# The first weight tile in halves of 256 columns, and GpSimd's bias tables placed behind the splits of x

## The chip, the core and the metric

The kernel runs on one core of a Trainium2 chip. The metric is the device time of one execution in microseconds, smaller is better. The engines of the core work side by side, each through its own list of instructions in order: TensorE (PE: matmuls, PEld: its weight loads), VectorE (DVE), ScalarE (ACT), GpSimd (POOL) and the DMA queues that ScalarE and SyncE (SP) issue to.

## The reference

One decoder layer on x (256 tokens, 1024 channels), all in float32:

```python
h = rms_norm(x, norm_g)
q, k, v, gate = split(h @ w_in, 4)          # w_in: 1024 x 4096
o = causal_attention(q, k, v, alibi)        # 16 heads of 64
x = x + (o * silu(gate)) @ w_out            # w_out: 1024 x 1024
return rms_norm(x, final_norm_g)
```

With 256 tokens there is one attention block of 256, so the block selection of the reference is plain causal attention with a linear distance penalty per head (ALiBi).

## The kernel before

**Split products.** TensorE multiplies in a reduced float32 format. To keep float32 accuracy each operand a is split into a high part (a rounded to that format) and a low part (a minus the high part), and a product is three matmuls: high·high, low·high, high·low. For weights ScalarE writes the high part `whi` by a copy, VectorE subtracts for the low part `wlo`. For x the transposed input `head` is scaled by the norm's gain: the high part `xh` is made by VectorE for k tiles 0 and 1 and by ScalarE for 2 to 7, the low part `xl` by VectorE in one instruction with two tensor inputs.

**Staging.** The 1024 input channels are 8 k tiles of 128. The weights come in pieces of 128 x 1024 elements. Pieces 0 to 3 hold the first half of the columns of v, two k tiles each (512 columns per k tile); later pieces hold 256 columns of q, k or the gate, four k tiles each. Four buffers hold weights as loaded, four their high parts and four their low parts.

**The first stage (v).** `run_first` multiplies all 8 k tiles into two banks: per k tile 6 matmuls of 512 columns. It picks the next matmul by a planner (`Plan`) that models when operands come, and before the first real one it issues warm-up matmuls on zeros (`warm_to`). The lists of all engines are fixed when the program is built.

**The norm's row scale.** h's division by the row norm is applied after the products. While the first stages run, ScalarE squares and sums two tiles of x (256 x 1024), VectorE turns each sum into a mean (`ms`), and GpSimd raises it to the power -1/2 (`rstd`, one instruction of 128 x 1 for each of the two row tiles). VectorE spreads each `rstd` along a diagonal (`spread`), TensorE transposes the two spread tiles (in the midst of the q matmuls), and ScalarE copies the result out as `rows`, with which q, k and the gate are scaled on their way out of their banks.

**The bias tables.** GpSimd computes the ALiBi penalty of each of the 16 heads, 128 x 256 elements (`make_bias`, one instruction per head from the table `dist`). The tables are first read by the softmax of the first head pair, after 33 us.

**Queues at the start.** ScalarE issues two transfers before its first instruction, SyncE all the others, in a written order. Lines that matter: `load` (172) and the calls at 182 to 188, `split_hi`/`split_lo` (230, 243), `make_bias` (218, called at 554), `root` (527, GpSimd's power at 534), `x_lo` (547), `v_first` (578), `fiber_norm` (602, the spread at 615).

Of the kernel before, what the change touches and what calls it, by code (L numbers as in the profile page):

```python
# [8 lines left out]
F32 = mybir.dt.float32  # L9
F32R = mybir.dt.float32r  # L10
AF = mybir.ActivationFunctionType
ALU = mybir.AluOpType

P = 128
S = 256
D = 1024
H = 16
DH = 64
NM = S // P
NK = D // P  # L20
CW = 512
GW = 256
KP = 4
# [9 lines left out]
N_PIECES = N_IN + NK  # L33


LAID = [("x", 0, 1), ("w", 0, 0, 2), ("x", 1, 2), ("w", 0, 1, 2)]
for c in range(1, NK // 2):
    LAID += [("x", 2 * c, 2 * c + 2), ("w", c, 0, 2), ("w", c, 1, 2)]
LAID += [("w", NK // 2, 0, 1)] + [("t", m) for m in range(NM)]
LAID += [("w", i, 0, 1) for i in range(NK // 2 + 1, N_PIECES)]  # L40
WIDTH, START = {}, {}
for seg in LAID:
    START[seg] = P * sum(WIDTH.values())
# [16 lines left out]
NL = 4  # L60
# [22 lines left out]
def f32(ap):  # L83
    return ap.bitcast(F32)
# [3 lines left out]
def trunk(ctx: ExitStack, tc, laid, fin_g, out):  # L88
    nc = tc.nc
    plan = Plan()  # L90
    const = ctx.enter_context(tc.tile_pool(name="const", bufs=1))
    w32p = ctx.enter_context(tc.tile_pool(name="w32p", bufs=NL))
    whp = ctx.enter_context(tc.tile_pool(name="whp", bufs=NW))
    wlp = ctx.enter_context(tc.tile_pool(name="wlp", bufs=NW))
# [11 lines left out]
    def mm(o, a, b, start, stop, n, dep=0.0):  # L106
        nc.tensor.matmul(o, a, b, start=start, stop=stop)  # L107
        return plan.mm(n, dep)
# [5 lines left out]
    def act(o, i, fn, n, dep, psum_in, scale=1.0, bias=0.0, accum=None):  # L114
        kw = {} if accum is None else {"accum_out": accum}
        if not isinstance(bias, float):
            kw["bias"] = bias
        nc.scalar.activation(o, i, fn, scale=scale, **kw)  # L118
        c = (50 if psum_in else 92) + n / 1.2
        c += 93 * ((not isinstance(scale, float)) + (not isinstance(bias, float)) + (accum is not None))  # L120
        return plan.op("act", c, dep)

    def dve(n, dep, rate=0.96, extra=0):
        return plan.op("dve", 66 + extra + n / rate, dep)
# [24 lines left out]
    gT, sg = head[:, :NK], head[:, NK:].rearrange("p (k n) -> p k n", k=NK)  # L149

    x_at, xt_at = [0.0] * NM, [0.0] * NK
    w32, whi, wlo, w_at, w_ready = {}, {}, {}, {}, {}
    dma = [1600.0]

    def fetch(o, seg, queue=None, dep=0.0):
        n = P * WIDTH[seg]
        (queue or nc.sync).dma_start(o, laid[START[seg]:START[seg] + n].rearrange("(p n) -> p n", p=P))
        dma[0] = max(dma[0], dep) + n / 90.0
        return dma[0] + LAT

    def load_x(m):

        x_at[m] = fetch(xs[m], ("t", m))

    def load_xt(k0, k1, queue=None):

        o = head[:, (NK + k0 * S if k0 else 0):NK + k1 * S]
        at = fetch(o, ("x", k0, k1), queue)
        for k in range(k0, k1):
            xt_at[k] = at  # L170

    def load(i, parts=1, dep=0.0, part=None, queue=None):
        if i >= N_PIECES:
            return
        if not part:
            w32[i] = w32p.tile([P, KP * GW], F32, name="w32")
            w_at[i] = []
        n = KP * GW // parts
        for u in range(parts) if part is None else [part]:
            w_at[i].append(fetch(w32[i][:, u * n:(u + 1) * n], ("w", i, u, parts), queue, dep))  # L180

    load_xt(0, 1)
    load(0, 2, part=0, queue=nc.scalar)
    load_xt(1, 2, nc.scalar)
    load(0, 2, part=1)
    for c in range(1, NK // 2):
        load_xt(2 * c, 2 * c + 2)
        load(c, 2)
# [1 line left out]

    ident = const.tile([P, P], F32, name="ident")
    make_identity(nc, ident)
    mhalf = const.tile([P, 1], F32, name="mhalf")
    nc.gpsimd.memset(mhalf, -0.5)
    dist = const.tile([P, S], F32, name="dist")
# [6 lines left out]
    x_hl = [const.tile([P, NK * S], F32R, name=f"x{t}") for t in "hl"]  # L202
    xh, xl = [[t[:, k * S:(k + 1) * S] for k in range(NK)] for t in x_hl]
# [14 lines left out]
    def make_bias(h):  # L218
        slope = -(2.0 ** (-8.0 * (h + 1) / H))
        nc.gpsimd.tensor_scalar(bias[:, h, :], dist, slope, 0.0, op0=ALU.mult, op1=ALU.add)  # L220


    nsplit = [0, 0]
    used_at = {}

    def rel(i):

        return used_at.get(N_IN if i == N_PIECES - 1 else i - NW + 1, 0.0) + 250.0

    def split_hi(parts=1, part=None):  # L230
        i = nsplit[0]
        if not part:
            whi[i] = x_hl[0][:, :KP * GW] if i == N_PIECES - 1 else whp.tile([P, KP * GW], F32R, name="whi")
            w_ready[i] = []
        n = KP * GW // parts
        for u in range(parts) if part is None else [part]:
            c = slice(u * n, (u + 1) * n)
            at = w_at[i][(u + 1) * len(w_at[i]) // parts - 1] if parts <= len(w_at[i]) else w_at[i][-1]
            w_ready[i].append(act(whi[i][:, c], w32[i][:, c], AF.Copy, n, max(at, rel(i)), False))
        if part is None or part == parts - 1:  # L240
            nsplit[0] += 1

    def split_lo(parts=None, part=None):
        i = nsplit[1]
        if not part:
            wlo[i] = x_hl[1][:, :KP * GW] if i == N_PIECES - 1 else wlp.tile([P, KP * GW], F32R, name="wlo")
        parts = parts or len(w_ready[i])
        n = KP * GW // parts
        for u in range(parts) if part is None else [part]:
            c = slice(u * n, (u + 1) * n)  # L250
            nc.vector.tensor_sub(wlo[i][:, c], w32[i][:, c], f32(whi[i][:, c]))  # L251
            w_ready[i][u] = dve(n, max(w_ready[i][u], rel(i)))
        if part is None or part == parts - 1:
            nsplit[1] += 1
            load(i + NL, 1, w_ready[i][-1] + 1100.0)

    used = [0, 0.0]

    def use(i):
        for u in range(used[0] + 1, i + 1):  # L260
            used_at[u] = plan.pe
        used[0] = i
        used[1] = plan.pe
        fill()
# [239 lines left out]
    with tc.manual_schedule():  # L504
# [10 lines left out]
        def warm_to(t):  # L515

            while plan.pe + 430.0 < min(t, WARM_END):
                warm(1)
# [18 lines left out]
        x_at_k = {}  # L537
# [11 lines left out]
                                           op0=ALU.mult, op1=ALU.subtract)  # L549
            x_at_k[k].append(dve(S, x_at_k[k][0], extra=62))  # L550

        whi_at = {}

        for h in range(H):
            make_bias(h)
        warm_to(3480.0)
        acc = banks[4:6]
        for b in acc:
            b["busy"] = True
        for c in range(NK // 2):  # L560
            for a in range(2):
                x_hi(2 * c + a, "act" if c else "dve")
                split_hi(2, a)
                x_lo(2 * c + a)
                whi_at.setdefault(c, []).append(w_ready[c][a])
                split_lo(2, a)
            if c == 0:
                load_x(0)
                load_x(1)

        def term(m, k, jj):
            i, a = divmod(k, 2)
            w_at_k = (whi_at if jj < 2 else w_ready)[i][a * len(w_ready[i]) // 2]
            return max(w_at_k, x_at_k[k][jj == 1])

        done = {0: 0, 1: 0}

        def v_first(m, k, jj):
            i, a = divmod(k, 2)
            xx, ww = ((xh, whi), (xl, whi), (xh, wlo))[jj]  # L580
            n = done[m]
            done[m] += 1
            return mm(acc[m]["t"], xx[k][:, m * P:(m + 1) * P], ww[i][:, a * CW:(a + 1) * CW], n == 0, n == 3 * NK - 1,
                      CW, term(m, k, jj))

        def run_first(todo, end=1e9):
            while todo and plan.pe < end:
                u = next((u for u in todo if term(*u) <= plan.pe), None) or min(todo, key=lambda u: term(*u))
                if term(*u) > end:
                    return  # L590
                warm_to(term(*u))
                todo.remove(u)
                r = v_first(*u)
                i = min([3] + [u[1] // 2 for u in todo])
                if i > used[0]:
                    use(i)
                fill()
                side()
                if done[u[0]] == 3 * NK:
                    evac("v", 0, u[0], acc[u[0]], r)  # L600

        def fiber_norm():
# [26 lines left out]
            have_rows.append(d)  # L629

        fibers.append([x_at[0], fiber_norm()])
        run_first([(m, k, jj) for k in range(NK) for jj in range(3) for m in range(NM)])
        nc.scalar.dma_start(gf, fin_g.unsqueeze(0).to_broadcast([P, D]))


        i = 3
        for kind, j in PARTS[1:]:
            acc = [take_now() for _ in range(2)]
            dep = [b["free"] for b in acc]
            w = CW if kind == "v" else GW  # L640
            kp = KP * GW // w
            for k in range(NK):
# [5 lines left out]
                for f in range(2):  # L648
                    fs = slice(f * P, (f + 1) * P)
                    for jj, (xx, ww) in enumerate(((xh, whi), (xl, whi), (xh, wlo))):  # L650
                        if kind == "v":
                            o, a, b = acc[f]["t"], xx[k][:, fs], ww[i][:, kk * w:(kk + 1) * w]
                        else:
                            o, a, b = acc[f]["t"][:, :S], ww[i][:, kk * w + f * P:kk * w + (f + 1) * P], xx[k]
# [33 lines left out]
        for m in range(NM):  # L688
# [4 lines left out]
            for u, (c0, c1) in enumerate(GROUPS[m]):  # L693
                c = slice(c0, c1)
# [63 lines left out]
```

## Time and profile before

| | before |
|---|---|
| time, median of 3 runs | 147.12 us (146.87 to 147.26) |
| the profiled execution's own time | 147.17 us |
| its span in the profile | 145.4 us |
| busy: TensorE | 138.4 us (95%) |
| busy: VectorE | 119.8 us (82%) |
| busy: ScalarE | 93.1 us (64%) |
| busy: GpSimd | 13.6 us (9%) |
| DMA | 24.83 MB, mean 171 GB/s |

The span is the time from the first to the last instruction that the profiler saw; the execution's own time is 1.77 us longer. The same instruction on the same shape appears with more than one duration in the rows below (the tables, the low parts, `rstd`); the single rows are therefore shown beside their groups.

### The profile page before, as it was taken

The numbers are of one execution on the slowest core, as the hardware profiler recorded it, in microseconds if no ns is written. First come the engines' busy times: TensorE is split into PE (matmuls) and PEld (weight loads), VectorE is DVE, ScalarE is ACT, GpSimd is POOL, SyncE is SP. The second block draws the span as 40 slices with busy tenths as digits, with TensorE's granted clock in tenths as the row PEclk, the third lists the DMA queues.
The fourth block names the chain that finished last, engine by engine and source line by source line (L and its number), as shares of the span: only waits on it lengthen the run. The fifth ranks groups of instructions, "written<-read, shape, count | busy, mean of one in ns | idle before, by whom it ended". The sixth has DMA issues, their size and how long they took to land.

```text
span 145.4 us, 2764 instructions
## 1 busy us (share of the span) xinstructions
PE 138.4 (95%) x1009; PEld 126.8 (87%) x1009; DVE 119.8 (82%) x291; ACT 93.1 (64%) x197; POOL 13.6 (9%) x29
## 2 busy tenths in 40 slices
PE   7999999999999999999999999999999999999930
PEld 5688899999999999999977789999899889888830
DVE  0999499888998996999999769877758999785870
ACT  3698977757976548976586867535596775531331
POOL 7891140000000000000000000000000000000210
PEclk9999999999999999999999999999999999999995
DMA  4999998596043264045476130875532134000123
GB/s 161 347 391 412 412 409 298 188 325 231 14 144 144 80 213 144 0 149 176 158 243 224 71 124 20 280 274 167 187 112 91 57 127 161 0 0 5 36 111 144
DMA packets 8078, 24.83 MB, mean 171 GB/s; under 512 B 896, under 2 KB 1408, under 8 KB 8064
## 3 DMA queue, kind: packets, MB, share of 16 engines
q1 hardware_dynamic: 7632, 23.73, 46.2%
q10 hardware_dynamic: 432, 0.92, 1.7%
q8 instruction: 8, 0.13, 0.4%
q14 instruction: 6, 0.05, 0.1%
HBM read 23.60 MB, written 1.05 MB: 170 GB/s over the span
## 4 chain that ended last, share of the span: by engine, by line
PE 89%; issue 3%; DMA 2%; DVE 1%; ACT 1%; POOL 1%; POOLq 0%
PE bank L107 81%; PE bank L348 5%; PE bank L111 4%; DMA w<-in_laid 2%; POOL fr L711 1%; DVE bias L702 1%; ACT bias L713 0%; POOLq L754 0%; DVE x L700 0%; ACT whi L118 0%; DVE fms L702 0%
## 5 line engine op out<-in xcount | busy, mean ns | idle before, releaser
L107 PE MATMUL bank<-xh,wlo 128*128 128x256 f32 x192 | 55.3, 288 | 0.0
L107 PE MATMUL bank<-xl,whi 128*128 128x256 f32 x192 | 55.1, 287 | 0.0
L107 PE MATMUL bank<-xh,whi 128*128 128x256 f32 x192 | 55.0, 287 | 0.0
L251 DVE TENSOR_TENSOR wlo<-w,whi 128x1024 fp32r<-128x1024 f32 (+1 forms) x43 | 48.9, 1142 | 6.7 <-ACT whi L118 6.7
L118 ACT ACTIVATE whi<-w 128x1024 fp32r<-128x1024 f32 (+1 forms) x43 | 41.8, 977 | 15.6 <-PE bank L107 7.9
L107 PEld LDWEIGHTS bank<-xh,whi 128*128 128x128 f32 x192 | 36.2, 189 | 0.3
L107 PEld LDWEIGHTS bank<-xh,wlo 128*128 128x128 f32 x192 | 36.2, 189 | 0.2
L107 PEld LDWEIGHTS bank<-xl,whi 128*128 128x128 f32 x192 | 36.2, 189 | 0.1
L118 ACT ACTIVATE pr<-st,mx 128x256 f32<-128x256 f32 (+1 forms) x32 | 14.1, 444 | 6.8 <-DVE mx L365 6.8
L107 PE MATMUL bank<-whi,ol 128*128 128x512 f32 (+1 forms) x35 | 12.7, 364 | 0.0
L711 POOL TENSOR_TENSOR fr<-fms,mhalf 128x1 f32<-128x1 f32 x2 | 1.6, 798 | 118.8 <-DVE fms L702 118.8
L107 PE MATMUL bank<-whi,oh 128*128 128x512 f32 (+1 forms) x35 | 12.7, 362 | 0.0
L107 PE MATMUL bank<-wlo,oh 128*128 128x512 f32 (+1 forms) x35 | 12.6, 359 | 0.0
L107 PE MATMUL bank<-whi,xh 128*128 128x512 f32 x32 | 12.3, 427 | 0.1
L111 PE MATMUL bank<-ident,pr 128*128 128x128 f32 x48 | 12.1, 272 | 0.0
L482 DVE TENSOR_TENSOR z<-bank,rows 128x256 f32<-128x256 f32 x24 | 9.4, 420 | 2.7 <-PE bank L107 2.6
L107 PE MATMUL bank<-whi,xl 128*128 128x512 f32 x32 | 11.6, 403 | 0.0
L107 PE MATMUL bank<-wlo,xh 128*128 128x512 f32 x32 | 11.6, 401 | 0.0
L118 ACT ACTIVATE pth<-bank 128x384 fp32r<-128x384 f32 x16 | 7.9, 492 | 4.1 <-PE bank L111 3.8
L365 DVE CUSTOM_DVE_ANT_0 st<-bank,bias 128x256 f32<-128x256 f32 (+1 forms) x32 | 9.8, 352 | 0.2 <-PE bank L348 0.2
L411 DVE TENSOR_TENSOR ptl<-bank,pth 128x384 fp32r<-128x384 f32 x16 | 8.8, 552 | 1.1 <-ACT pth L118 1.1
L107 PE MATMUL bank<-ptl,vv 128*128 128x256 f32 (+1 forms) x32 | 8.9, 278 | 0.0
(81 smaller groups left out, 210.1 us busy)
## 6 DMA issues: line engine op xcount, KB each, us to landing
w<-in_laid SPq DMA_DIRECT2D x36, 512.0 KB, 4.1
w<-in_laid SPq DMA_DIRECT2D x7, 256.0 KB, 5.0
x<-in_laid SPq DMA_DIRECT2D x2, 512.0 KB, 6.8
head<-in_laid SPq DMA_DIRECT2D x3, 256.0 KB, 5.1
out<-bias SPq DMA_DIRECT2D x2, 320.0 KB, 2.3
gf<-in_fin_g ACTq DMA_DIRECT2D x1, 512.0 KB, 5.5
out<-bias SPq DMA_DIRECT2D x2, 192.0 KB, 1.9
w<-in_laid ACTq DMA_DIRECT2D x1, 256.0 KB, 3.1
```

The costliest lines, as they stand in the source:

```text
L107: nc.tensor.matmul(o, a, b, start=start, stop=stop)
L111: nc.tensor.transpose(o, a, ident)
L118: nc.scalar.activation(o, i, fn, scale=scale, **kw)
L251: nc.vector.tensor_sub(wlo[i][:, c], w32[i][:, c], f32(whi[i][:, c]))
L348: nc.tensor.matmul(bs[a]["t"][:, c], u[rr, m * P:(m + 1) * P], w[rr, 0:c.stop - c.start], start=jj == 0, stop=jj == 2)
L365: nc.vector.tensor_tensor_reduce(st[:, a, c0:c1], ps, bt, scale=-1.0, scalar=BIG, op0=ALU.add, op1=ALU.min, accum_out=mx[:, cc:cc + 1])
L411: nc.vector.tensor_sub(lo[:, a], pv, f32(hi[:, a]))
L482: nc.vector.tensor_mul(z, ps, rows8 if kind == "q" else rows)
L702: nc.vector.tensor_tensor_reduce(sq[:, :c1 - c0], y[:, c], y[:, c], scale=1.0 / D, scalar=ms[:, u - 1:u], op0=ALU.mult, op1=ALU.add, accum ...
L711: nc.gpsimd.tensor_tensor(r, ms[:, ns - 1:ns], mhalf, op=ALU.pow)
```

## The change

Four things change, all in the first 22 us or so.

1. Piece 0's first k tile (512 columns) is loaded as two transfers of 256 columns, the first on ScalarE's queue, the second on SyncE's. Piece 0's second k tile goes to ScalarE's queue, x's second k tile to SyncE's.
2. The splits of that k tile (`whi`, `wlo`) are two instructions of 256 columns each, and its 6 matmuls are 12 of 256 columns.
3. The 16 bias tables are issued behind the last low part of x: GpSimd first copies one column of `xl` of k tile 7 into `junk`, so the tables wait for VectorE to have written it.
4. The planner sees its first operands earlier and places 5 warm-up matmuls in place of 7.

```diff
-LAID = [("x", 0, 1), ("w", 0, 0, 2), ("x", 1, 2), ("w", 0, 1, 2)]
+LAID = [("x", 0, 1), ("w", 0, 0, 4), ("w", 0, 1, 4), ("w", 0, 1, 2), ("x", 1, 2)]
...
     load_xt(0, 1)
-    load(0, 2, part=0, queue=nc.scalar)
-    load_xt(1, 2, nc.scalar)
-    load(0, 2, part=1)
+    load(0, 4, part=0, queue=nc.scalar)
+    load(0, 4, part=1)
+    load(0, 2, part=1, queue=nc.scalar)
+    load_xt(1, 2)
...
-        for h in range(H):
-            make_bias(h)
         warm_to(3480.0)
...
                 x_hi(2 * c + a, "act" if c else "dve")
-                split_hi(2, a)
+                cuts = [slice(0, GW), slice(GW, CW)] if c + a == 0 else [slice(a * CW, (a + 1) * CW)]
+                for u in cuts:
+                    hi_part(c, u)
                 x_lo(2 * c + a)
-                whi_at.setdefault(c, []).append(w_ready[c][a])
-                split_lo(2, a)
+                for u in cuts:
+                    lo_part(c, u)
...
+        nc.gpsimd.tensor_copy(junk, f32(xl[NK - 1][:, 0:1]))
+        for h in range(H):
+            make_bias(h)
...
+            nc.tensor.matmul(acc[m]["t"][:, u], xx[k][:, m * P:(m + 1) * P],
+                             ww[i][:, a * CW + u.start:a * CW + u.stop], start=n == 0, stop=done[m] == 3 * D * CW // P,
+                             skip_group_check=True)
...
-        run_first([(m, k, jj) for k in range(NK) for jj in range(3) for m in range(NM)])
+        whole, parts = [slice(0, CW)], [slice(0, GW), slice(GW, CW)]
+        run_first([(m, k, jj, u) for k in range(NK) for jj in range(3) for u in (whole if k else parts)
+                   for m in range(NM)])
```

`hi_part` and `lo_part` issue the same copy and subtraction as `split_hi` and `split_lo`, on the columns given.

GpSimd's list before, from the table `dist` to the powers at the end of the kernel (`rstd` is the row scale of the norm, `fr` that of the final norm):

```order
L197 AFFINE_SELECT dist<-dist 128x256
L220 TENSOR_SCALAR bias<-dist 128x256 x16
L534 TENSOR_TENSOR rstd_145<-ms,mhalf 128x1
L534 TENSOR_TENSOR rstd_146<-ms,mhalf 128x1
L711 TENSOR_TENSOR fr<-fms,mhalf 128x1 x2
```

The same stretch of GpSimd's list after the change:

```order
L200 AFFINE_SELECT dist<-dist 128x256
L588 COPY junk<-xl 128x1
L223 TENSOR_SCALAR bias<-dist 128x256 x16
L524 TENSOR_TENSOR rstd_147<-ms,mhalf 128x1
L524 TENSOR_TENSOR rstd_148<-ms,mhalf 128x1
L735 TENSOR_TENSOR fr<-fms,mhalf 128x1 x2
```

The order among tables and powers is the same; what is new is the copy in front of the tables, which waits for VectorE's last `xl`.

ScalarE's list at the start, before (-) and after (+); `w_106` is piece 0 as loaded:

```order
+L157 DMA w_106<-in_laid 128x256
 L157 DMA w_106<-in_laid 128x512
-L157 DMA head<-in_laid 128x256
 L118 ACT_TABLE_LOAD
-L118 ACTIVATE whi<-w_106 128x512 x2
+L118 ACTIVATE whi<-w_106 128x256 x2
+L118 ACTIVATE whi<-w_106 128x512
 L118 ACTIVATE xh<-head 128x256
```

The first copy of the weights needs only 256 columns now, and the transfer of x's second k tile has left this queue.

VectorE's list after the change around the spread of the row scale (in brackets whose semaphore an instruction waits for); the order is that of before:

```order
L242 TENSOR_TENSOR wlo<-w_188,whi 128x1024 [waits DMAHW1_49,PE_49,Activation_49]
L519 TENSOR_SCALAR ms<-ss 128x1
L521 SCALAR_TENSOR_TENSOR ms<-ss,ms 128x1 [waits DVE_49]
L242 TENSOR_TENSOR wlo<-w_200,whi 128x1024 [waits DMAHW2_49,PE_49,Activation_49]
L637 TENSOR_SCALAR spread<-ident,rstd_147 128x128 [waits Pool_49]
L637 TENSOR_SCALAR spread<-ident,rstd_148 128x128 [waits Pool_49]
L242 TENSOR_TENSOR wlo<-w_212,whi 128x1024 [waits DMAHW4_49,PE_49,Activation_49]
```

Nothing moved here, and TensorE's two transposes of the spread tiles stand at the same place in its list too, behind the same 43 matmuls of the q stage.

## Rows read from the trace of the kernel before

**Rows 1.** The page's first part: busy us, share of the span, instructions.

```profile
PE 138.4 (95%) x1009; PEld 126.8 (87%) x1009; DVE 119.8 (82%) x291; ACT 93.1 (64%) x197; POOL 13.6 (9%) x29
```

**Rows 2.** The chain that ended last: start us, us, what.

```profile
3.80 0.64 ACT whi L118
4.48 17.14 PE bank L107 x91
```

**Rows 3.** Windows of TensorE: stretch, us, busy (instructions), granted clock, DMA share, GB/s.

```profile
22.00:32.00 10.00, 10.00 (x89) 1.00 0.77 263
...
122.00:132.00 10.00, 10.00 (x55) 1.00 0.11 44
```

**Rows 4.** Timeline of TensorE: start us, us, engine, line, operation, [idle before <-releaser].

```profile
1.03 0.80 PE L511 MATMUL bank<-oh 128*128 128x512 f32 x1 [1.03 <-DVE eps_t L212]
1.63 0.63 PE L511 MATMUL bank<-oh 128*128 128x512 f32 x1
2.06 0.63 PE L511 MATMUL bank<-oh 128*128 128x512 f32 x1
...
6.08 0.63 PE L107 MATMUL bank<-wlo,xh 128*128 128x512 f32 x2
6.55 0.63 PE L107 MATMUL bank<-whi,xh 128*128 128x512 f32 x2
...
21.46 0.38 PE L111 MATMUL bank<-ident,spread 128*128 128x128 f32 x2
```

**Rows 5.** Timeline of VectorE, 3 to 21 us, same columns.

```profile
3.46 0.53 DVE L544 TENSOR_SCALAR xh<-head 128x256 fp32r<-128x256 f32 x1 [2.47 <-DMA head<-in_laid]
4.50 0.88 DVE L251 TENSOR_TENSOR wlo<-w,whi 128x512 fp32r<-128x512 f32 x1
...
11.13 0.62 DVE L548 SCALAR_TENSOR_TENSOR xl<-head,xh 128x256 fp32r<-128x256 f32 x1
...
12.68 0.68 DVE L251 TENSOR_TENSOR wlo<-w,whi 128x512 fp32r<-128x512 f32 x1
13.28 0.47 DVE L548 SCALAR_TENSOR_TENSOR xl<-head,xh 128x256 fp32r<-128x256 f32 x1
...
17.88 1.22 DVE L251 TENSOR_TENSOR wlo<-w,whi 128x1024 fp32r<-128x1024 f32 x1 [2.06 <-ACT whi L118]
...
19.32 1.23 DVE L251 TENSOR_TENSOR wlo<-w,whi 128x1024 fp32r<-128x1024 f32 x1
...
20.99 0.29 DVE L615 TENSOR_SCALAR spread<-ident,rstd 128x128 f32<-128x128 f32 x1 [0.24 <-POOL rstd L534]
```

**Rows 6.** Timeline of ScalarE, 10 to 12 us, same columns.

```profile
10.82 0.64 ACT L118 ACTIVATE whi<-w 128x512 fp32r<-128x512 f32 x1
11.36 0.49 ACT L118 ACTIVATE xh<-head 128x256 fp32r<-128x256 f32 x1
```

**Rows 7.** Timeline of GpSimd: all 16 tables as one row, then single ones, then `rstd`.

```profile
2.04 9.44 POOL L220 TENSOR_SCALAR bias<-dist 128x256 f32<-128x256 f32 x16
3.44 0.40 POOL L220 TENSOR_SCALAR bias<-dist 128x256 f32<-128x256 f32 x1
3.90 0.40 POOL L220 TENSOR_SCALAR bias<-dist 128x256 f32<-128x256 f32 x1
4.90 0.74 POOL L220 TENSOR_SCALAR bias<-dist 128x256 f32<-128x256 f32 x1
...
10.74 0.74 POOL L220 TENSOR_SCALAR bias<-dist 128x256 f32<-128x256 f32 x1
15.91 0.56 POOL L534 TENSOR_TENSOR rstd<-ms,mhalf 128x1 f32<-128x1 f32 x1 [4.43 <-DVE ms L531]
19.45 1.50 POOL L534 TENSOR_TENSOR rstd<-ms,mhalf 128x1 f32<-128x1 f32 x1 [2.98 <-DVE ms L531]
```

**Rows 8.** Windows of TensorE at the end of the kernel, columns as in the third group.

```profile
139.00:140.00 1.00, 0.54 (x5) 1.00 0.15 56
...
142.00:143.00 1.00, 0.00 (x0) 0.64 0.30 106
```

More of the change, by code (lines that the diff above doesn't have):

```diff
@@ L151, in trunk @@
     x_at, xt_at = [0.0] * NM, [0.0] * NK
-    w32, whi, wlo, w_at, w_ready = {}, {}, {}, {}, {}
+    w32, whi, wlo, w_at, w_cols, w_ready = {}, {}, {}, {}, {}, {}
     dma = [1600.0]
@@ L176, in load @@
             w32[i] = w32p.tile([P, KP * GW], F32, name="w32")
-            w_at[i] = []
+            w_at[i], w_cols[i] = [], []
         n = KP * GW // parts
@@ L180, in load @@
             w_at[i].append(fetch(w32[i][:, u * n:(u + 1) * n], ("w", i, u, parts), queue, dep))
+            w_cols[i].append(n)
     load_xt(0, 1)
-    load(0, 2, part=0, queue=nc.scalar)
-    load_xt(1, 2, nc.scalar)
-    load(0, 2, part=1)
+    load(0, 4, part=0, queue=nc.scalar)
+    load(0, 4, part=1)
+    load(0, 2, part=1, queue=nc.scalar)
+    load_xt(1, 2)
     for c in range(1, NK // 2):
@@ L192, in trunk @@
     make_identity(nc, ident)
+    junk = const.tile([P, 1], F32, name="junk")
     mhalf = const.tile([P, 1], F32, name="mhalf")
@@ L228, in rel, with split_hi, split_lo @@
         return used_at.get(N_IN if i == N_PIECES - 1 else i - NW + 1, 0.0) + 250.0
-    def split_hi(parts=1, part=None):
+    def split_hi():
         i = nsplit[0]
[L232 to L243, printed above, removed]
-        i = nsplit[1]
[L245 to L255, printed above, removed]
+        whi[i] = x_hl[0][:, :KP * GW] if i == N_PIECES - 1 else whp.tile([P, KP * GW], F32R, name="whi")
+        w_ready[i] = [act(whi[i], w32[i], AF.Copy, KP * GW, max(w_at[i][-1], rel(i)), False)]
+        nsplit[0] += 1
+    def split_lo():
+        i = nsplit[1]
+        wlo[i] = x_hl[1][:, :KP * GW] if i == N_PIECES - 1 else wlp.tile([P, KP * GW], F32R, name="wlo")
+        nc.vector.tensor_sub(wlo[i], w32[i], f32(whi[i]))
+        w_ready[i] = [dve(KP * GW, max(w_ready[i][0], rel(i)))]
+        nsplit[1] += 1
+        load(i + NL, 1, w_ready[i][-1] + 1100.0)
     used = [0, 0.0]
@@ L550, in x_lo, with arrival, hi_part, lo_part @@
             x_at_k[k].append(dve(S, x_at_k[k][0], extra=62))
-        whi_at = {}
-        for h in range(H):
-            make_bias(h)
+        hi_at, lo_at = {}, {}
+        def arrival(i, u):
+            n = 0
+            for w, at in zip(w_cols[i], w_at[i]):
+                n += w
+                if n >= u.stop:
+                    return at
+        def hi_part(i, u):
+            if u.start == 0:
+                whi[i] = whp.tile([P, KP * GW], F32R, name="whi")
+            hi_at[i, u.stop - 1] = act(whi[i][:, u], w32[i][:, u], AF.Copy, u.stop - u.start, arrival(i, u), False)
+            if u.stop == KP * GW:
+                w_ready[i] = [hi_at[i, u.stop - 1]]
+                nsplit[0] += 1
+        def lo_part(i, u):
+            if u.start == 0:
+                wlo[i] = wlp.tile([P, KP * GW], F32R, name="wlo")
+            nc.vector.tensor_sub(wlo[i][:, u], w32[i][:, u], f32(whi[i][:, u]))
+            lo_at[i, u.stop - 1] = dve(u.stop - u.start, hi_at[i, u.stop - 1])
+            if u.stop == KP * GW:
+                w_ready[i] = [lo_at[i, u.stop - 1]]
+                nsplit[1] += 1
+                load(i + NL, 1, w_ready[i][-1] + 1100.0)
         warm_to(3480.0)
@@ L569, in trunk, with term, v_first @@
                 load_x(1)
-        def term(m, k, jj):
+        nc.gpsimd.tensor_copy(junk, f32(xl[NK - 1][:, 0:1]))
+        for h in range(H):
+            make_bias(h)
+        def term(m, k, jj, u):
             i, a = divmod(k, 2)
-            w_at_k = (whi_at if jj < 2 else w_ready)[i][a * len(w_ready[i]) // 2]
-            return max(w_at_k, x_at_k[k][jj == 1])
+            return max((lo_at if jj == 2 else hi_at)[i, a * CW + u.stop - 1], x_at_k[k][jj == 1])
         done = {0: 0, 1: 0}
-        def v_first(m, k, jj):
+        def v_first(m, k, jj, u):
             i, a = divmod(k, 2)
@@ L581, in v_first @@
             n = done[m]
-            done[m] += 1
-            return mm(acc[m]["t"], xx[k][:, m * P:(m + 1) * P], ww[i][:, a * CW:(a + 1) * CW], n == 0, n == 3 * NK - 1,
-                      CW, term(m, k, jj))
+            done[m] += u.stop - u.start
+            nc.tensor.matmul(acc[m]["t"][:, u], xx[k][:, m * P:(m + 1) * P],
+                             ww[i][:, a * CW + u.start:a * CW + u.stop], start=n == 0, stop=done[m] == 3 * D * CW // P,
+                             skip_group_check=True)
+            return plan.mm(u.stop - u.start, term(m, k, jj, u))
         def run_first(todo, end=1e9):
@@ L598, in run_first @@
                 side()
-                if done[u[0]] == 3 * NK:
+                if done[u[0]] == 3 * D * CW // P:
                     evac("v", 0, u[0], acc[u[0]], r)
```

## The prediction

> **What bounds the kernel now.** I read the page's busy shares first: TensorE 95%, the others well below [rows 1]. Then the chain of waits in time: it starts with the first copy of weights on ScalarE (3.80 us, 0.64) and hands over to TensorE at 4.48, with 91 matmuls in one piece [rows 2]. Then TensorE by windows: busy 10.00 of 10 us in every one of the eleven windows from 22 to 132 us [rows 3]. So a microsecond that TensorE loses anywhere before 132 us is lost at the end; no later gap gives it back. The timeline of TensorE splits the start in two. [...] There are no gaps from 6.08 on. The early change can thus shift only what lies before 6.08.
>
> The second place is further on: at 21.46 TensorE transposes the two spread tiles [rows 4], and that needs VectorE's second spread, at 20.99 after a wait for `rstd` [rows 5], and that needs both powers of GpSimd, the second from 19.45 to 20.95 [rows 7]. TensorE works through its list in order, so a late `rstd` stops it there. Before, `rstd` was in time by about 0.2 us.
>
> **Part 1: the halves.** Before, TensorE starts when ScalarE has copied 512 columns (3.80 + 0.64). `head` lands by 3.46 [rows 5], the 256 KB of weights by 3.80. A quarter of 128 KB lands between these two; I take 3.45, near `head`, which has nearly its size. A copy of 256 columns lies between nothing and the 0.49 of a scaled copy of that width [rows 6]; I take 0.42. `xh` on VectorE takes 0.53 beside the tables [rows 5], and no less than the 0.29 of a spread of half the width; I take 0.38. So the start moves from 4.48 to about 3.95 (bounds 3.80 and 4.45). These 0.53 us are run at the low clock, so they are worth 0.53 x 0.235/0.43 = 0.3 us (0 to 0.4). The 12 halves in place of 6 matmuls carry the same columns; I cost them at nothing, hidden by the same streaming (at most 0.1).
>
> **Part 2: VectorE without the tables.** With tables beside them a low part of weights takes 0.88 and of x 0.62; without, 0.68 and 0.47 [rows 5]. That saves 0.35 us per k tile on VectorE. TensorE had no gap in this stage, so by itself the saving is worth nothing; it only keeps the 0.3 us of part 1 from being waited away.
>
> **Part 3: the tables behind the splits.** Moved past: the two powers. They stand behind the 16 tables in GpSimd's list, before and after, but the tables ended at 11.48 before, with 4.4 us to spare. Now:
>
> - Start. ScalarE is the slower of the two split engines once VectorE is relieved. The high part of the last x tile ends at 11.36 + 0.49 = 11.85 and the weights' copy before it at 11.46 [rows 6]; VectorE then does a low part of weights (0.68, to 12.14) and the last `xl` (0.47): 12.6. The copy into `junk` stands beside one more low part of weights (0.68) and a GpSimd instruction that meets one waits for it (next point), so the first table starts at about 13.2 (bounds 12.7 and 13.4).
> - Pitch. Alone, tables follow each other every 0.46 us (3.44, 3.90). Beside VectorE's splits the ten starts from 4.90 to 10.74 make nine steps of 0.65 us [rows 7]: VectorE issues one instruction per 0.67 us there (a low part of weights and one of x in 1.34), so GpSimd gets one table in per VectorE instruction, and one is stretched from 0.40 to 0.74. The short power at 19.45 says the same: it takes 0.56 alone and 1.50 beside the long split of 19.32 to 20.55, and ends 0.4 behind it [rows 5, 7].
> - Sum. Between the last `xl` and the first spread VectorE's list holds three splits of 1024 columns, 1.22 us each [rows 5]. Each holds GpSimd for about 1.0 us. 13.2 + 16 x 0.465 + 3 x 1.0 = 23.6 us for the last table. The two powers, alone now since VectorE waits for them: 2 x 0.55 = 1.1, but the first spread fits beside the second power; then the second spread, 0.3: 25.0, and some 0.1 for the signals: the transposes at 25.1 instead of 21.46.
>
> [...]
>
> Cost: TensorE arrives at the transposes 0.3 us earlier than before, so part 1 only lengthens the wait. Queued behind them is all the rest of TensorE's list. On VectorE the next split is queued behind the spreads, on ScalarE the evacuation of v waits for the same `rstd`; they shift by about the same 3.6 us as TensorE does, so I charge them little. The bias tables are done ten microseconds before their first reader.
>
> **Sum.** From the profiled execution: 147.17 + (25.1 - 21.46) = 150.8; and 0.2, chosen and not read, for what VectorE has to catch up: 151.0. Its own time lies 0.05 above the median of the three runs, so 151.0 stands for these too. Bounds of the third part: all tables at 0.46 with nothing between, start 12.7, transposes at 12.7 + 7.4 + 1.4 = 21.5 (no change); all at 0.65 and start 13.4, 13.4 + 10.4 + 1.4 = 25.2, with one more held split 26.2 (+4.7).
>
> **Rivals.**
>
> - *The clock falls in the wait.* TensorE would stand still from about 21.2 to 25.1. At the end of the kernel its last matmul is over at 139.54, and the granted clock, 1.00 until 142, averages 0.64 in the next microsecond: it fell at about 142.3, 2.7 us after the last matmul [rows 8]. A wait of 3.9 us is longer. At the start TensorE worked from 1.03 and had the fast pitch by 6.08 [rows 4]: at most 5.0 us at 0.43 for 0.235. So a fall costs up to 5.0 x (1 - 0.235/0.43) = 2.3 us, and half of that if the rise comes sooner. Time 152.1 to 153.3, say 152.7. Against it: a single fall is seen, and GpSimd may be done earlier. [...] No run here shows it inside a kernel yet.
> - [...] If a table goes on at 0.46/0.74 = 0.6 of its pace beside a split that is stretched to some 1.5 us, the three splits cost 3 x 0.6 = 1.8 us rather than 3.0: transposes at 23.9, time 149.6. For it: only splits of 512 columns are seen beside tables; against it the 1.50 us power.
> - *Faster.* The tables are done in time and part 1 reaches the end: 147.17 - 0.3 = 146.8. This decides if the last table ends by 19.7, since 1.4 us follow before the transposes at 21.1. From 13.2 that is 0.41 us per table, below the 0.46 of the undisturbed ones, or a start at 11.2 with the held splits left out. Nothing in the rows supports either.
> - *No change.* The move costs about what part 1 gives: last table at about 20.1, time 147.1. It needs the undisturbed pitch throughout and the earliest start.
>
> **How the numbers follow.** Forecast, a wait of 3.5 to 4.1 us at full clock, 151.0 (150.3 to 151.6): 0.46. Clock falls, 152.7: 0.28. Better sharing, 149.6 (148.5 to 150.3): 0.16. No change, 0.05. Faster, 0.05. A change within 0.3% (0.44 us) can't be told from none with this kernel. Range 149.2 to 153.1: it leaves out the last two cases and the lower edge of the sharing. Faster 0.05, same 0.05, slower 0.90.
>
> **What would show it.** In the profile after: TensorE's first real matmul at about 3.9 to 4.0; low parts of 0.68 and 0.47 through the whole first stage; GpSimd idle until about 13, then 16 tables to about 23.6, stretched past 1 us where a split of 1024 columns runs; `rstd` behind them; VectorE's first spread with a long wait for GpSimd; a gap of nearly 4 us on TensorE ahead of the transposes. After it matmuls of 256 columns every 0.12 us mean that the clock held, every 0.21 that it fell. The forecast is wrong if the tables end before 20 us, or if TensorE passes the transposes without a gap; the size is wrong by the clock, or if tables run beside the long splits.

## The result and the profile after

The changed kernel takes 151.81 us (median of 6 runs), the one before 147.25 (6 runs taken with them): a ratio of 1.030 with a 95% interval of 1.0269 to 1.0331, slower by 4.4 us by this ratio and 4.6 between the medians. Four slow runs (154.33 of the changed kernel, 153.35 of the tables alone, and 763.91 and 779.69, one each of two kernels further on) are left out of the ratios, though not of the medians. The other five of the changed kernel took 151.08 to 152.89 us, with a median of 151.44. The ratios and intervals are those on record; they weigh all compared runs and need not be the quotients of the medians. The profiled execution took 152.18 us, its span is 150.4 us.

The chain of waits, which was one piece of 91 matmuls from 4.48 us on [rows 2], now goes through GpSimd (start us, us, what):

```profile
14.30 1.27 POOL bias L223
...
23.59 1.05 POOL rstd L524 x2
25.02 0.47 PE bank L111
25.49 10.92 PE bank L107 x82
```

The tables, the two powers of the row scale, VectorE's second spread (24.67 to 24.96, shown below) and the second transpose follow each other with less than 0.1 us between them, and TensorE goes on behind it. The page puts 8% of the chain on GpSimd. GpSimd's own timeline (start us, us, engine, line, operation, [idle before <-releaser]), to be set against [rows 7]:

```profile
12.71 0.58 POOL L588 COPY junk<-xl 128x1 f32<-128x1 f32 x1 [10.76 <-DVE xl L538]
13.37 10.23 POOL L223 TENSOR_SCALAR bias<-dist 128x256 f32<-128x256 f32 x16
13.83 0.41 POOL L223 TENSOR_SCALAR bias<-dist 128x256 f32<-128x256 f32 x1
14.30 1.27 POOL L223 TENSOR_SCALAR bias<-dist 128x256 f32<-128x256 f32 x1
...
17.98 1.48 POOL L223 TENSOR_SCALAR bias<-dist 128x256 f32<-128x256 f32 x1
19.52 1.37 POOL L223 TENSOR_SCALAR bias<-dist 128x256 f32<-128x256 f32 x1
...
23.56 1.08 POOL L524 TENSOR_TENSOR rstd<-ms,mhalf 128x1 f32<-128x1 f32 x2
```

13 of the 16 tables take 0.40 or 0.41 us, three are stretched to 1.27, 1.48 and 1.37, one for each of VectorE's three splits of 1024 columns; each of the three ends 0.26 or 0.27 us behind its split. The last table ends at 23.6. VectorE, against [rows 5]:

```profile
10.13 0.48 DVE L538 SCALAR_TENSOR_TENSOR xl<-head,xh 128x256 fp32r<-128x256 f32 x1
10.53 0.69 DVE L562 TENSOR_TENSOR wlo<-w,whi 128x512 fp32r<-128x512 f32 x1
...
14.03 1.28 DVE L242 TENSOR_TENSOR wlo<-w,whi 128x1024 fp32r<-128x1024 f32 x1 [0.78 <-ACT whi L118]
...
17.97 1.23 DVE L242 TENSOR_TENSOR wlo<-w,whi 128x1024 fp32r<-128x1024 f32 x1 [1.92 <-ACT whi L118]
...
19.40 1.22 DVE L242 TENSOR_TENSOR wlo<-w,whi 128x1024 fp32r<-128x1024 f32 x1
24.15 0.29 DVE L637 TENSOR_SCALAR spread<-ident,rstd 128x128 f32<-128x128 f32 x1 [3.53 <-POOL rstd L524]
24.67 0.29 DVE L637 TENSOR_SCALAR spread<-ident,rstd 128x128 f32<-128x128 f32 x1 [0.23 <-POOL rstd L524]
```

The early splits are relieved as meant (0.48 and 0.69 where it was 0.62 and 0.88); the price is the wait of 3.53 us ahead of the first spread. TensorE, against [rows 4]:

```profile
1.03 2.50 PE L501 MATMUL bank<-oh 128*128 128x512 f32 x5 [1.03 <-DVE eps_t L215]
3.84 1.72 PE L603 MATMUL bank<-whi,xh 128*128 128x256 f32 x4 [0.31 <-ACT whi L118]
...
7.07 0.94 PE L603 MATMUL bank<-whi,xh 128*128 128x512 f32 x2
7.85 0.63 PE L603 MATMUL bank<-whi,xl 128*128 128x512 f32 x2
8.32 0.63 PE L603 MATMUL bank<-wlo,xh 128*128 128x512 f32 x2
...
22.18 0.28 PE L107 MATMUL bank<-xh,whi 128*128 128x256 f32 x1
24.49 0.33 PE L111 MATMUL bank<-ident,spread 128*128 128x128 f32 x1 [2.03 <-DVE spread L637]
25.02 0.47 PE L111 MATMUL bank<-ident,spread 128*128 128x128 f32 x1 [0.19 <-DVE spread L637]
25.14 0.56 PE L107 MATMUL bank<-xl,whi 128*128 128x256 f32 x1
...
25.71 0.41 PE L107 MATMUL bank<-xh,whi 128*128 128x256 f32 x1
25.93 0.41 PE L107 MATMUL bank<-xl,whi 128*128 128x256 f32 x1
...
28.26 0.28 PE L107 MATMUL bank<-xh,whi 128*128 128x256 f32 x1
28.38 0.28 PE L107 MATMUL bank<-xl,whi 128*128 128x256 f32 x1
```

Three things are to be seen. TensorE starts earlier (3.84 for 4.48), but k tile 1 comes later: 7.07 instead of 6.55, because the fast pitch (two matmuls of 512 columns in 0.47) is there only from 7.85. At the transposes it stands still for 2 us. And behind them the matmuls of 256 columns follow each other every 0.21 us until 28.26, then every 0.12: the clock had fallen. The windows of TensorE say the same, with a granted clock of 0.50 from 25 to 28 us (stretch, us, busy, granted clock, DMA share, GB/s):

```profile
23.00:24.00 1.00, 0.00 (x0) 1.00 0.63 250
24.00:25.00 1.00, 0.33 (x1) 0.91 0.08 33
25.00:26.00 1.00, 0.98 (x5) 0.50 0.00 0
...
28.00:29.00 1.00, 1.00 (x10) 0.88 0.51 201
...
32.00:42.00 10.00, 10.00 (x94) 1.00 0.69 212
```

From 29 us on the engine is as full as before [rows 3]. The account of this execution: the first matmul behind the transposes comes at 25.14 where the same one came at 21.60 before, 3.5 us; some 14 matmuls then follow each other every 0.213 instead of 0.119 us, 1.3 us; together 4.8 of the 5.0 us by which 152.18 exceeds 147.17.

### The profile page after: what moved, and what is told of

Read it like the earlier page. It is cut to its first block, busy times and chain, and to the rows that moved or that the text cites. A ratio compares the mean times of both kernels' runs of the same rounds, so it can differ in the third digit from the quotient of the medians.

```text
span 150.4 us, 2777 instructions
## 1 busy us (share of the span) xinstructions
PE 140.8 (94%) x1013; PEld 129.0 (86%) x1013; DVE 118.8 (79%) x292; ACT 93.2 (62%) x198; POOL 14.0 (9%) x30
## 4 chain that ended last, share of the span: by engine, by line
PE 76%; POOL 8%; issue 4%; DMA 3%; DVE 3%; SPq 2%; ACT 1%; POOLq 0%
PE bank L107 67%; POOL bias L223 6%; PE bank L338 4%; PE bank L111 4%; DMA w<-in_laid 3%; SPq L157 2%; DVE xl L538 1%; DVE wlo L562 1%; POOL rstd L524 1%; POOL fr L735 1%; DVE bias L726 0%; ACT bias L737 0%; POOLq L778 0%; DVE x L724 0%; ACT whi L118 0%
## 5 line engine op out<-in xcount | busy, mean ns | idle before, releaser
L107 PE MATMUL bank<-xh,wlo 128*128 128x256 f32 x192 | 55.9, 291 | 0.0
L107 PE MATMUL bank<-xl,whi 128*128 128x256 f32 x192 | 55.9, 291 | 0.0
L118 ACT ACTIVATE whi<-w 128x1024 fp32r<-128x1024 f32 (+2 forms) x44 | 41.9, 959 | 17.6 <-PE bank L107 7.8
L242 DVE TENSOR_TENSOR wlo<-w,whi 128x1024 fp32r<-128x1024 f32 x35 | 42.6, 1221 | 8.5 <-ACT whi L118 8.5
L107 PEld LDWEIGHTS bank<-xh,wlo 128*128 128x128 f32 x192 | 36.9, 192 | 0.2
L107 PEld LDWEIGHTS bank<-xh,whi 128*128 128x128 f32 x192 | 36.9, 192 | 0.3
L107 PEld LDWEIGHTS bank<-xl,whi 128*128 128x128 f32 x192 | 37.0, 193 | 0.1
L223 POOL TENSOR_SCALAR bias<-dist 128x256 f32<-128x256 f32 x16 | 9.3, 587 | 0.9
L118 ACT ACTIVATE cs<-bank 64x512 f32<-64x512 f32 x8 | 4.8, 595 | 6.5 <-PE bank L107 6.5
L107 PE MATMUL bank<-pth,vv 128*128 128x256 f32 (+1 forms) x32 | 8.1, 252 | 0.0
```

Source lines behind the costliest of these rows:

```text
L242: nc.vector.tensor_sub(wlo[i], w32[i], f32(whi[i]))
```

## Experiments

Two theories stood against each other after the profile. *Queue*: the tables in front of the two powers hold the row scale back, and TensorE waits for it; the clock that falls in the wait adds to it. *Start*: the halves and the warm-ups left out lose time in the first microseconds. The trace showed signs of both.

**The tables alone** (the kernel before, all tables behind the splits):

```diff
-        for h in range(H):
-            make_bias(h)
         warm_to(3480.0)
...
+        nc.gpsimd.tensor_copy(junk, f32(xl[NK - 1][:, 0:1]))
+        for h in range(H):
+            make_bias(h)
```

> The kernel before with one part of the change: all 16 tables behind the last low part of x, weights loaded and multiplied as before. Queue theory (the tables in front of the two powers hold the row scale back until about 24.6 us, TensorE stands at the transposes): last table at 23.4 to 23.8, the transposes at about 25.0 in place of 21.46, so 150.7 at full clock and up to 152.3 where the clock falls in the wait; the whole loss of the change is here. Rival (the halves or the two warm-ups fewer lose part of the time at the start, where the changed kernel's k tile 1 came at 7.07 instead of 6.55): this kernel lies 0.5 to 1.0 below the changed one.

Measured 152.33 us (before: 147.14), ratio 1.030 (1.0247 to 1.0355), the same ratio as the whole change: the loss comes with the tables, and the halves make no difference clear of the noise. The second transpose stands at 25.21 behind waits of 2.99 and 0.19 us, and the clock falls in this execution as it did above (mean granted clock 0.981 where the fastest of this kernel has 0.992):

```profile
24.69 0.33 PE L111 MATMUL bank<-ident,spread 128*128 128x128 f32 x1 [2.99 <-DVE spread L618]
```

**The other part alone** (the changed kernel, tables back at their place ahead of the warm-ups):

> The other part alone: the changed kernel with the 16 tables back at their old place. Queue theory: no wait at the transposes, tables done at 11 to 12 us; 146.8 to 147.3, since part 1 is worth 0.3 at most and the tables slow xh by 0.15 again. Rival (the start loses): the first matmul comes at 4.0 but the fast pitch only after 7 us, and it is 147.7 to 148.2.

Measured 148.78, ratio 1.0085 (1.0057 to 1.0113), a loss of 1.3 us by the ratio and 1.6 by the medians: the rival holds, with a median 0.6 above its range. TensorE's timeline of this run:

```profile
4.16 1.44 PE L602 MATMUL bank<-whi,xh 128*128 128x256 f32 x4 [0.62 <-ACT whi L118]
...
7.95 1.05 PE L602 MATMUL bank<-whi,xl 128*128 128x512 f32 x2
8.81 0.82 PE L602 MATMUL bank<-wlo,xh 128*128 128x512 f32 x2
9.46 0.63 PE L602 MATMUL bank<-whi,xh 128*128 128x512 f32 x2
```

Two matmuls still take 0.86 us (the slow pitch) until 8.8; the first pair at the fast pitch stands at 9.46, 3.4 us later than before. There is no wait at the transposes, which come 1.5 us late.

**Tables in three places** (the changed kernel with 2 tables in front, 8 behind the splits, 6 behind the second power):

```diff
+        for h in range(2):
+            make_bias(h)
         warm_to(3480.0)
...
         nc.gpsimd.tensor_copy(junk, f32(xl[NK - 1][:, 0:1]))
-        for h in range(H):
+        for h in range(2, 10):
             make_bias(h)
...
             nc.gpsimd.tensor_tensor(rstd[m], ms[m][:, 1:2], mhalf, op=ALU.pow)
+            if m == NM - 1:
+                for h in range(10, H):
+                    make_bias(h)
```

> The changed kernel with the tables in three places: 2 in front as before, 8 behind the splits of x, 6 behind the second power. Queue theory: the second power ends at about 21.0 as before, no wait at the transposes, the halves keep what they gain: 146.7 to 147.2. Rival 1 (the six tables beside VectorE's splits from 21 to 25 make the k splits late for the scores): a gap of 0.3 to 0.8 ahead of the first score matmuls, 147.4 to 147.9. Rival 2 (the start loses): 147.7 to 148.2.

Measured 148.39, ratio 1.0088 (1.0059 to 1.0116): the wait at the transposes is gone (TensorE passes them at 23.13 without idling), and what is left is the late start of the run above. TensorE shows no wait behind the transposes, so the six tables behind the powers cost it none. With the queue put right, 3.4 us of the change's loss come back and 1.2 remain.

```profile
23.13 0.38 PE L111 MATMUL bank<-ident,spread 128*128 128x128 f32 x2
```

**Zeros in the wait** (the changed kernel, 13 matmuls on zeros ahead of the transposes):

> The changed kernel with 13 matmuls of 512 columns on zeros ahead of the two transposes (2.8 us at the fast pitch), so that TensorE stands still for less than 1 us there. If the clock's fall is part of the loss: the pitch behind the transposes is 0.12 in every profile, and the runs gather at 150.7 to 151.1, 0.7 to 1.0 below the changed kernel's median. If the wait alone is the loss: no difference from the changed kernel, 151.5 to 152. If the zeros push the transposes back: above 152.

Measured 151.82, as the changed kernel: inconclusive. The clock held (mean granted clock 0.988 to 0.996 in the four executions), but TensorE reached the zeros only at 23.15 and they pushed the transposes to 26.15 (3.0 us for the 13, 0.23 each, where I had put 2.8), 0.6 us behind the end of the second spread (25.27 + 0.29), so one gain paid for another loss. Repeated below on a kernel that arrives earlier.

**Which part of the start?** Seven warm-ups with the tables in three places, and five with the kernel before. The first edit is shown, beside that of the tables in three places; the second leaves the first two warm-ups out of TensorE's list and nothing else:

```diff
+        for _ in range(2):
+            nc.tensor.matmul(banks[7]["t"].rearrange("p (a n) -> p a n", n=P), zr,
+                             zr.unsqueeze(1).to_broadcast([P, CW // P, P]), start=True, stop=True)
         warm_to(3480.0)
```

> The tables in three places (2, 8 and 6) and the halves, with 7 warm-ups in place of 5, so that TensorE has no gap ahead of the first half. Gap theory (the fast pitch came at about 9 us with the halves and at 5.8 before, because TensorE stood still from 3.33 to 4.0 and again between the halves): fast pitch by 6 us, 146.7 to 147.3, 1.1 to 1.7 below the same kernel with 5 warm-ups. Rival (the halves themselves, their short matmuls or the second half's late transfer, keep the clock low): 148.0 to 148.8 as with 5.

> The kernel before with 2 warm-ups left out and nothing else: whole columns, first real matmul at 4.48, a gap from 3.33 to 4.48 on TensorE. Gap theory: the fast pitch comes late (7.5 to 9.3 us), 147.9 to 149.0. Rival (the halves are the cause): as before, 147.0 to 147.4.

Seven: 147.84, ratio 1.0046 (1.0022 to 1.007), 0.55 below the same kernel with five, half of what the gap theory asked for. Five, with whole columns: 148.2, ratio 1.007 (1.0034 to 1.0106). So the two missing warm-ups cost about 1.1 us in a kernel that is otherwise the one before, and the time and the late fast pitch are those of the gap theory:

```profile
4.44 1.22 PE L107 MATMUL bank<-whi,xh 128*128 128x512 f32 x2 [0.90 <-ACT whi L118]
...
8.02 0.97 PE L107 MATMUL bank<-whi,xl 128*128 128x512 f32 x2
8.82 0.63 PE L107 MATMUL bank<-wlo,xh 128*128 128x512 f32 x2
```

With seven, the halves and the tables in three places the fast pitch is there by 5.5, but TensorE then waits: at 8.14 it stood 0.64 us for ScalarE's copy of k tile 2, and ScalarE had waited for a transfer:

```profile
6.84 0.51 ACT L118 ACTIVATE xh<-head 128x256 fp32r<-128x256 f32 x1 [1.70 <-DMA head<-in_laid]
7.46 0.63 ACT L118 ACTIVATE whi<-w 128x512 fp32r<-128x512 f32 x1
```

My 146.7 to 147.3 for this kernel was too low by half a microsecond.

**Half of the tables behind the splits** (kernel before, 8 in front, 8 behind):

> The kernel before with 8 tables at the old place and 8 behind the last low part of x. Queue theory: the 8 end at about 18.0, the two powers at 18.5 and 21, no wait at the transposes: 146.9 to 147.4, a difference of under 0.3 from before. Rival (any table beside the long splits delays the row scale): a gap at the transposes of 0.5 or more, 147.6 or above.

Measured 147.65 (before, taken with it: 147.08), ratio 1.0028 (1.0003 to 1.0053); in the profiled execution, 147.25, TensorE passes the transposes at 21.50 without a wait. So the loss is small, 0.3% with an interval that just leaves out none, and nothing is gained by the relief of VectorE. The median of 147.65 is above the forecast and lies at the rival's bound, but in the one execution with a trace its gap isn't there; what the slower ones lose stays open.

**The clock's share** (all tables behind, whole columns, seven warm-ups, 12 matmuls on zeros ahead of the transposes):

> All 16 tables behind the splits, whole columns, 7 warm-ups, and 12 matmuls of 512 columns on zeros (2.7 us) ahead of the transposes. TensorE reaches them at 21.5 and is done with the zeros before 24.7, so nothing is pushed back. Clock theory: the matmuls behind the transposes keep the pitch of 0.12; every run at 150.3 to 151.0, where the same kernel without the zeros had 150.4 to 153.4 and a median of 152.3: 1.3 to 1.8 less. Rival (the wait alone is the loss): the same median and the same spread.

Measured 150.61, ratio 1.022 (1.0187 to 1.0258), 1.7 us below the median of the same kernel without the zeros; the compared runs lie within 150.3 to 150.62. TensorE's timeline and what follows the transposes:

```profile
22.11 2.93 PE L627 MATMUL bank<-oh 128*128 128x512 f32 x12
24.89 0.40 PE L111 MATMUL bank<-ident,spread 128*128 128x128 f32 x2
...
25.25 0.28 PE L107 MATMUL bank<-xh,wlo 128*128 128x256 f32 x1
25.36 0.28 PE L107 MATMUL bank<-xh,whi 128*128 128x256 f32 x1
```

The pitch behind them is 0.12 at once, and the granted clock reads 1.00 in every window from 22 to 28 us. TensorE came to the zeros at 22.11 and not at 21.5, but VectorE's second spread ended only at 24.90 (24.61 + 0.29), so the zeros did not push the transposes back. So the late row scale costs 3.5 us (150.61 - 147.08) with the clock held. The 1.7 us between the medians is not the clock alone: the first matmul behind the transposes stands at 25.04 here and at 25.29 in the trace without zeros, and not every execution without zeros shows the fall (next section).

**Twelve tables behind the splits:**

> The kernel before with 4 tables at the old place and 12 behind the last low part of x: a third point between 8 (no wait) and 16 (a wait of 3.3 us at the transposes). Queue theory: the last four tables stood alone at 0.47 us each, so the twelfth ends at about 22.0, the transposes come at 23.3 to 23.6 with a gap of 1.6 to 2.1 us; 148.8 to 149.4 at full clock, and since the gap is shorter than the 2.7 us after which the clock was seen to fall, few runs above 149.8. Rival (the loss goes with the clock, not with the number of tables): 150.5 or more, or no loss.

Measured 149.0 (148.85 to 149.09; before 147.41), ratio 1.0099 (1.0076 to 1.0122). The third point lies where the count puts it: by the medians 8 tables lose 0.6 us (0.4 by the ratio), 12 lose 1.6 and 16 lose 3.5 at full clock. The gap is shorter than expected, 1.2 us for 1.6 to 2.1; TensorE was late itself (it reached the transposes at about 21.65), and the second transpose, 23.36, is where it was put. GpSimd's last table and the first power, then TensorE:

```profile
21.53 0.40 POOL L221 TENSOR_SCALAR bias<-dist 128x256 f32<-128x256 f32 x1
21.90 0.56 POOL L535 TENSOR_TENSOR rstd<-ms,mhalf 128x1 f32<-128x1 f32 x1
```

```profile
22.84 0.33 PE L111 MATMUL bank<-ident,spread 128*128 128x128 f32 x1 [1.03 <-DVE spread L620]
23.36 0.33 PE L111 MATMUL bank<-ident,spread 128*128 128x128 f32 x1 [0.19 <-DVE spread L620]
...
23.64 0.28 PE L107 MATMUL bank<-xh,wlo 128*128 128x256 f32 x1
23.76 0.28 PE L107 MATMUL bank<-xh,whi 128*128 128x256 f32 x1
```

After this shorter wait the pitch stays at 0.12, and the mean granted clock of the four executions (0.987 to 0.998) is that of the kernel before.

**The whole change with seven warm-ups:**

> The whole change with 7 warm-ups in place of 5. Theory (what the missing warm-ups lose at the start is hidden in the wait for the row scale, which GpSimd ends at the same time): TensorE reaches the transposes at 21.2 to 21.7 instead of 22.3, the transposes stay at 24.7 to 25.2, the gap is 3.2 to 3.8; no gain, 151.0 to 152.6. Rival (start and wait add up): 1.1 less than the change, 150.0 to 150.8.

Measured 152.61, ratio 1.031 (1.0268 to 1.0356): no gain over the change with five (151.81). TensorE has the fast pitch from 6 us and reaches the transposes 0.4 us earlier (21.9 for 22.3), but they do not stand where they stood:

```profile
25.01 0.33 PE L111 MATMUL bank<-ident,spread 128*128 128x128 f32 x1 [2.96 <-DVE spread L640]
25.53 0.33 PE L111 MATMUL bank<-ident,spread 128*128 128x128 f32 x1 [0.20 <-DVE spread L640]
```

Both are 0.5 us later than in the changed kernel (24.49 and 25.02), since the tables start at 13.86 instead of 13.37: ScalarE got k tile 2 of x at 6.40 instead of 5.94, and the last `xl` starts at 12.66 instead of 12.17. That a repaired start is worth nothing therefore rests on the times more than on this trace: the one execution here whose mean granted clock is not low (0.990) took 151.16, those of the changed kernel 151.08 to 151.44.

**The halves alone, seven warm-ups:**

> The halves alone, tables at the old place, 7 warm-ups: what the halves are worth without the gap at the start. If they give the 0.3 of the forecast: 146.7 to 146.9. If the transfers of k tiles 2 and 3 take it back (ScalarE waited until 6.8 for them in two runs): 147.0 to 147.8, with a wait of TensorE for ScalarE's copy of k tile 2. If halves cost by themselves: above 148.

Measured 147.62 (before 147.41), ratio 1.0012 (0.9996 to 1.0028): no difference. In its profile the first matmul stands at 4.19, 0.29 us earlier than before, and k tile 1 at 6.55 exactly as before [rows 4]:

```profile
6.55 0.63 PE L605 MATMUL bank<-whi,xh 128*128 128x512 f32 x2
```

ScalarE waited for a transfer ahead of four of its first five instructions, longest (0.84 us) for the second half; its copy ended at 4.91, and TensorE's third matmul, due at about 4.6, stands at 4.96. TensorE did not wait for k tile 2, as I had expected, and its transposes stand at 21.45 where they stood at 21.46.

No version beat the kernel before; the nearest are the last one and the 8 tables behind the splits, 0.1% and 0.3% slower by their ratios, the first not clear of the noise.

## Why the prediction was right, and where it was not

- **The mechanism and its place** were right: tables ahead of the powers in GpSimd's list, the spread late, TensorE standing at the transposes. Tables alone show the same loss as the whole change; tables in three places take the wait away; the count of tables scales it.
- **The sum for the tables** was right to 0.1 us: 23.6 forecast for the last table, 23.6 measured; the second power done at 24.6, the second transpose at 25.0 for the forecast 25.1. What carried it was reading a table as *held* for a whole VectorE instruction: one per long split, 3 x 1.0 us, measured 0.87 + 1.07 + 0.96 (beyond the 0.40 or 0.41 of a table alone), each of the three ending 0.26 or 0.27 us behind its split. The traces show these times, not what holds a table. Part of the accuracy is luck: the tables started 0.2 us later than forecast and ran 0.2 us shorter. Tables that go on at 0.6 of their pace beside the splits, the case forecast at 149.6, would have ended near 22.4 (my estimate, 13.2 + 16 x 0.465 + 3 x 0.6).
- **The loss by the late row scale**, without the clock, was forecast at 3.6 to 3.8 us; with the clock held it measures 3.5 (150.61). The 0.2 us added for VectorE's catching up is shown by no run: in the trace with zeros the first matmul behind the transposes is 3.4 us late (25.04 for 21.60), and the whole execution too (150.52 for 147.17).
- **The clock** was a rival with a chance of 0.28, up to 2.3 us. The forecast set it against the case at full clock, but both happen, in different executions of one kernel. The record gives the mean granted clock of each. In the three kernels with all tables behind the splits and no zeros (the change, the tables alone, the change with seven warm-ups) the 12 compared executions make two groups: five at 0.990 to 0.992 took 150.42 to 151.44 us, seven at 0.980 to 0.985 took 152.18 to 152.89. Three of the seven have traces, and all three show the fall; no compared execution of any other kernel is below 0.986. So of the changed kernel three executions came out as forecast at full clock (150.3 to 151.6) and two as forecast for the fall (152.1 to 153.3); that the median lies between the groups, where no execution is, comes from the mixture. Within a kernel the groups' means lie 1.3, 1.9 and 1.5 us apart, which is the price of a fall here. I argued from the 2.7 us after which it fell at the end [rows 8]; here it fell by 25 us, after TensorE had stood still from 22.4 and done no more than one transpose at 24.49, so that figure is no bound. Why it falls in one execution and not in the next stays open.
- **What the halves do at full clock** stays open too. With all tables behind and the clock held, the four executions with the halves and no zeros took 151.08 to 151.44 us; those without halves (one of the tables alone, four with the zeros) took 150.30 to 150.62.
- **The step that failed is part 1:** "worth 0.3 us", reckoned from the pitches of [rows 4], 0.43 us per 512 columns from 1.63 to 2.06 and 0.47 for two such matmuls from 6.08. I priced the start at 3.95 (measured 3.84) and the copy at 0.42 (0.42), but gave the two warm-ups left out no price at all, although the change lists them. Without them TensorE idles ahead of the first real matmul (0.31 us in the changed kernel, 0.90 with whole columns) and the first pair at the fast pitch comes at 7.85 to 9.63 us instead of 6.08: by the medians +1.6 us with the tables in place, +1.1 with whole columns. With seven warm-ups the halves are worth nothing measurable either: the first matmul is earlier, k tile 1 is not, as the second half's transfer comes late. The sum came out all the same, by luck, because the loss fell into the wait: TensorE came to the transposes at 22.3, not at 21.1, the gap there was 2.2 us and not the nearly 4 that were forecast, and the end is set by GpSimd. The change with seven warm-ups agrees: the start is repaired, the time isn't.
- **VectorE's relief** was priced at nothing, and 8 tables behind the splits, which give part of it without the wait, gain nothing (0.3% slower).

## What to carry to other kernels

Work moved to an idle stretch of an engine is still in front of everything that this engine's list holds behind it: before moving 16 short instructions, look for the next instruction on that engine that somebody waits for, and put it first (here the second power ended at 24.6 where it had ended at 20.95; no run here puts all 16 behind the powers; six behind them, in the run with the tables in three places, took the wait away). Price a move onto GpSimd by how many splits VectorE has in the new stretch, not by a mean pitch: here each of three splits of 1024 columns held one table, for 0.87 to 1.07 us. And when a change lets real work start earlier, count the filler matmuls that it removes: two fewer, with the gap that they left, cost 1.1 us here with whole columns, and with the halves, whose first matmul came 0.32 us earlier (4.16 for 4.48), the loss was 1.6 by the medians.

## What the runs showed of the hardware

The fast pitch of TensorE at the start comes later with two warm-ups fewer. With 7 warm-ups up to the first real matmul the first group at the fast pitch (0.235 us per 512 columns) stood between 5.0 and 7.2 us in every profile; with 5, and 0.31 to 1.1 us of idling ahead of and among the first real matmuls, between 7.85 and 9.63. Until then 512 columns take 0.43 us. That the clock is what changes there is my reading of the pitch: behind the transposes of the changed kernel 256 columns took 0.213 us, the same pace, where the granted clock reads 0.50, but at the start that column shows 1.00 from 1 to 7 us in the trace of before. Whether the idling or the smaller number of warm-ups delays the fast pitch is not separated here.

Around the transposes the clock fell, by the mean granted clock (0.980 to 0.985 where it fell, 0.990 to 0.992 where not), in seven of the 12 executions whose kernels wait there for 2.2 to 3.2 us in their traces, at a price of 1.3 to 1.9 us each; it fell in none of the four whose kernel waits 1.2 us (0.987 to 0.998), and in none of the eight with zeros in the wait (0.987 to 0.997). In the trace of the change with seven warm-ups it fell only at about 26.3, when TensorE was at work again since 25.53: five matmuls at 0.12 us came first, then the slow pitch. The fall does not come in every execution with such a wait: five of the 12 took 150.42 to 151.44 us without it.

GpSimd's copy of a single element per partition took 0.58 us behind `xl`, beside a split of VectorE (12.57 to 13.25). That it was held there fits the powers (0.56 alone and 1.5 beside a split), but no run shows the copy alone.
